# The recurrence's convolution and gates as float32 products on TensorE, on unsplit data

## The chip, the cores and the metric

The kernel runs on one core of a Trainium2 chip. The metric is the device time of one execution in microseconds (us). The core has four compute engines that matter here: TensorE (PE, with PEld for its weight loads), VectorE (DVE), ScalarE (ACT) and GpSimd (POOL); SyncE (SP) issues the transfers. Each engine takes its instructions in the order of its own queue.

## What is computed

One step of a layer with two groups of heads that share one input: `x + W_out [a recurrence | sparse attention](norm(x) W_in)`, then `x + SwiGLU(norm(x))`. There are 1024 new rows of one stream and 8 x 16 rows of eight running streams, together 1152 rows in 9 tiles of 128, with a width of 1024. Cut to what the change touches, the recurrence is:

```python
def causal_conv(xr, prev, w, b):
    xpad = jnp.concatenate([prev, xr], axis=1)
    y = b
    for j in range(4):
        y = y + xpad[:, j:j + T] * w[j]          # one weight per tap and channel
    return y, xpad[:, -3:]

def rglru(x, pos, h_prev, ...):                  # x = causal_conv(...), 512 channels in 8 blocks of 64
    r = sigmoid(x_block @ w_rg + b_rg)
    i = sigmoid(x_block @ w_ig + b_ig)
    a = exp(-8 * r * softplus(-lru_lambda))
    h = scan(a, sqrt(1 - a * a) * i * x)         # along time, from h_prev
```

The other group takes queries, keys and values with rotary embedding, an indexer that scores every key, the best 256 (or a quarter) of them for every row, and softmax attention over those.

## The kernel before

Everything is held with channels or rows on the 128 partitions. Large products are split: a float32 operand becomes a high and a low part in the reduced type `fp32r`, and a product is three matmuls (`mm3`: high with high and the two mixed ones). `mm4` (line 207 on) is one float32 matmul on unsplit operands; before the change a few products of the index stage (`ps<-yF`) use it.

The stages follow one another: norm and k/v projections (to 71 us in the profiled execution), indexer scores (to 184), the recurrence ("lru", to about 389 with its tail), the query projection (`q_proj`, to 435), the recurrence's half of the output projection (`out_tile` with key "wa", to 500), attention (to 682), the attention half of the output ("wb", to 742) and the feed-forward part.

The recurrence runs in eight units, for each of 4 columns of 128 channels one `lru_main` ("m") and one `lru_gate` ("g"). A unit goes over the 1152 rows in 3 thirds of 384. In `lru_main` a third t is projected (24 `fp32r` matmuls, `ps<-h,w`), ACT copies the result to `xp` behind the three rows ahead of it (t = 2 holds 256 rows of the long stream and eight short streams of 16 rows, each with its own three rows), ACT writes tap 3 and the bias to `xc`, and DVE adds taps 0 to 2 with one `scalar_tensor_tensor` each (six in t = 2). `split` then makes `xh`: the high part on ACT, the low part on POOL. The gate weights come by DMA to `braw` and are split to `bd` on POOL. `gates` makes two `mm3` products `ps<-xh,bd` for a third, ACT makes `tr`, `ti`, `tt` from them, DVE and ACT work these into the coefficients, and three scans on DVE (`tr<-tt,tr,ti`) close a column and write its last state to `tail`. Tiles `xc`, `ti`, `tt` come from one ring of 8 (`LRU_C`); a column uses nine, so that those of one column wait for the scans of the column before.

`lru_out` transposes `tail` on PE (`ps<-ident,tail`) after the last column, and DVE copies the result to `to`. `q_proj` has 18 units of 24 matmuls (`ps<-w,h`), 432 in all; `out_tile` "wa" has 216 matmuls (`ps<-w,rest`, `ps<-smr,rest`, `ps<-rest`).

Beside these stages run side jobs. `topk` finds thresholds by counting: for one group of tiles ACT counts (with Sign), for the other DVE counts (`jk<-key,tk_cnt`), and DVE does the arithmetic between the counts (`tk_cand`, `tk_cnt`) and at last the masks. `k_rope` turns the keys (`kn<-kn,tab`, `rp<-kn`, `kn<-kn,rp`, `kn<-kn,kss`, 9 tiles), writes them out and stacks their transposes; its scratch (`gk`, `tab`, `rp`) lies in pool "woa" of the phase "wa". A planner (`run`, `step`, `fill`) sets the order in which the program is written; top-k steps are written with a priority lowered by 400. Then the program is scheduled anew by list scheduling, `TileContext(nc, schedule_with_timeline_sim=True)`, which sets each engine's final order. Pools of SBUF are stacks: a pool opened later takes the place of one that was closed, and what is written there waits for the last use of what lay there.

Of the kernel before, what the change touches and what calls it, by code (L numbers as in the profile page):

```python
# [9 lines left out]
F32 = mybir.dt.float32  # L10
F32R = mybir.dt.float32r
# [3 lines left out]
AF = mybir.ActivationFunctionType  # L15
# [66 lines left out]
class Kernel:  # L82
# [124 lines left out]
    def mm4(self, out, lhsT, rhs, start, stop):  # L207

        self.pe += 4 * rhs.shape[1] / 2400.0
        self.nc.tensor.matmul(out, lhsT, rhs, start=start, stop=stop)  # L210
# [192 lines left out]
    XH = 3  # L403
    XP = 2
    BD = 1
# [623 lines left out]
    def lru_main(self, n, c, lp):  # L1029
# [8 lines left out]
        braw = self.raw.tile([128, 2, 128], F32, tag="raw", name="braw")  # L1038
        nc.gpsimd.memset(braw, 0.0)
        for k, nm in ((0, "w_rg"), (1, "w_ig")):  # L1040
            for s in range(2):
                nc.sync.dma_start(braw[64 * s:64 * s + 64, k, 64 * s:64 * s + 64], I[nm][2 * c + s])
        bd = lp.tile([128, 2, 2, 128], F32R, tag="bd", name="bd", bufs=self.BD)
        self.hi(bd[:, :, 0, :], braw, "pool")
        self.lo(bd[:, :, 1, :], braw, bd[:, :, 0, :], "pool")
        xps, xhs, xcs, G = [], [], [], []
        trs = []

        def claim(k):
            while self.c_free < k:  # L1050
                yield 0.3
            self.c_free -= k

        def conv(t, px):
            self.begin()
            xc = third("xc")
            xcs.append(xc)
# [7 lines left out]
            xs = xp[:, 259:411].rearrange("p (b j) -> p b j", b=NB)  # L1065
            if t == 2:
                S.activation(xs[:, :, 3:19], px[:, 256:384].rearrange("p (b j) -> p b j", b=NB), AF.Copy)
                nc.gpsimd.tensor_scalar(xs[:, :, 0:3], prm[:, c, 16:40].rearrange("p (b j) -> p b j", b=NB), 1.0, 0.0,
                                        op0=ALU.mult, op1=ALU.add)
            xps.append(xp)  # L1070
            S.activation(xc, px[:, :384], AF.Identity, scale=prm[:, c, 3:4], bias=prm[:, c, 4:5])
            for j in range(3):
                wj = prm[:, c, j:j + 1]
                o = xc[:, :n]
                V.scalar_tensor_tensor(o, xp[:, j:j + n], wj, o, op0=ALU.mult, op1=ALU.add)
                if t == 2:
                    o = xc[:, 256:384].rearrange("p (b j) -> p b j", b=NB)
                    V.scalar_tensor_tensor(o, xs[:, :, j:j + 16], wj, o, op0=ALU.mult, op1=ALU.add)
            if t == 2:
                nc.gpsimd.tensor_scalar(tail[:, c, 0:3], xp[:, 256:259], 1.0, 0.0, op0=ALU.mult, op1=ALU.add)  # L1080
                nc.gpsimd.tensor_scalar(tail[:, c, 3:27].rearrange("p (b j) -> p b j", b=NB), xs[:, :, 16:19], 1.0, 0.0,
                                        op0=ALU.mult, op1=ALU.add)
            xh = lp.tile([128, 2, 384], F32R, tag="xh", name="xh", bufs=self.XH)
            self.split(xh, xc, "act", "pool")
            xhs.append(xh)
            return self.end() + self.LRU_LAT

        def gates(t):
            xh, xc = xhs[t], xcs[t]
# [4 lines left out]
            for k, dst in ((0, tr), (1, ti)):  # L1094
                pg = self.ps()
                self.mm3(pg[:, :384], bd[:, k, 0, :], bd[:, k, 1, :], xh[:, 0], xh[:, 1], True, True)
                S.activation(dst, pg[:, :384], AF.Tanh, scale=0.5, bias=hb[:, c, k:k + 1])
# [5 lines left out]
        for t in range(3):  # L1103
            px = self.ps()
            yield from self.proj_T(px[:, :384], w, self.h[t])
            yield from claim(1)
            ready.append(conv(t, px))
# [638 lines left out]
```

## Time and profile before

| | us |
|---|---|
| median of 3 runs (1569.49 to 1570.11) | 1569.83 |
| the profiled execution, its own time | 1569.72 |
| its span (1.8 us lie around it) | 1567.9 |
| PE busy in the span | 1446.7 |
| DVE busy | 916.7 |
| ACT busy | 626.2 |
| POOL busy | 312.8 |

The page gives the busy time of each engine, the span in 40 slices (39.2 us each) with the busy share in tenths, and the chain of work that ended last. PE bears 72% of that chain and DVE 18%. The slices tell which engine is full where: slices 5 to 12 (about 196 to 510 us) are DVE's, the rest is PE's.

### The profile page before, as it was taken

The page shows a single profiled execution, that of the slowest core. Times are in us where ns is not written, and L with a number is a line of the kernel's source. Part 1 is how long each engine was busy: PE and PEld are TensorE (multiplying, and loading weights), DVE is VectorE, ACT ScalarE, POOL GpSimd, SP SyncE. Part 2 cuts the span into 40 slices and gives each one's busy share as a digit, 9 for nine tenths or more (in the row PEclk, how much of TensorE's full clock was granted, in tenths as well). Part 3 has the DMA queues.
Part 4 walks back from the last instruction along what each step waited for, and adds up shares of the span by engine and source line. Part 5 has one row for each costly group of instructions (what it writes and reads, how often), then busy time and mean ns, then how long its engine had stood idle before and what let it go on. Part 6 is the DMA issues. An engine that isn't in the chain of part 4 may idle for free.

```text
span 1567.9 us, 20857 instructions
## 1 busy us (share of the span) xinstructions
PE 1446.7 (92%) x7754; PEld 1322.8 (84%) x7754; DVE 916.7 (58%) x1957; ACT 626.2 (40%) x1481; POOL 312.8 (20%) x453
## 2 busy tenths in 40 slices
PE   6889887756888999999999999999999999999998
PEld 6777777746766788888999999999898989898987
DVE  7556899999999888768324233333324242424143
ACT  6457968875633978655302020202120212111110
POOL 4215225541986434400000000000000000000000
PEclk8999898877898999999999999999999999999999
DMA  7201101100320002121202020202020201111003
GB/s 239 56 16 42 35 16 29 29 27 14 134 71 22 1 14 57 39 68 42 81 13 81 1 81 0 81 0 81 1 81 15 67 28 54 41 41 54 28 1 121
DMA packets 93797, 74.65 MB, mean 48 GB/s; under 512 B 13236, under 2 KB 84532, under 8 KB 93696
## 3 DMA queue, kind: packets, MB, share of 16 engines
q1 hardware_dynamic: 93696, 73.32, 15.5%
q8 instruction: 61, 1.00, 0.3%
q14 instruction: 40, 0.33, 0.1%
HBM read 67.03 MB, written 6.27 MB: 47 GB/s over the span
## 4 chain that ended last, share of the span: by engine, by line
PE 72%; DVE 18%; ACT 4%; issue 3%; DMA 1%; POOL 1%; SPq 0%; POOLq 0%; ACTq 0%; DVEq 0%
PE ps L205 67%; DVE jk L66 7%; PE ps L215 4%; DVE tk_cand L66 2%; DVE tr L66 1%; DVE xc L66 1%; ACT jk L66 1%; DVE qn L66 1%; DVE ti L66 1%; PE ps L210 1%; DVE tk_cnt L66 1%; DVE s L66 1%; DVE kn L66 0%; ACT relu L66 0%; DVE acc L66 0%
## 5 line engine op out<-in xcount | busy, mean ns | idle before, releaser
L205 PE MATMUL ps<-hf,w 128*128 128x384 f32 x2556 | 460.6, 338 | 0.0
L205 PEld LDWEIGHTS ps<-hf,w 128*128 128x128 f32 x2556 | 451.5, 187 | 0.8
L205 PE MATMUL ps<-w,a 128*128 128x512 f32 x999 | 239.1, 390 | 0.0
L66 DVE TENSOR_TENSOR acc<-ps,acc 128x512 f32<-128x512 f32 x234 | 161.3, 690 | 119.7 <-PE ps L205 119.2
L205 PEld LDWEIGHTS ps<-w,a 128*128 128x128 f32 x999 | 187.3, 188 | 40.1
L66 DVE TENSOR_TENSOR sg<-ps,sg 128x384 f32<-128x384 f32 x66 | 36.8, 557 | 281.7 <-PE ps L205 281.1
L66 ACT ACTIVATE w<-raw 128x512 fp32r<-128x512 f32 x128 | 77.7, 629 | 300.9 <-PE ps L205 220.0
L66 DVE TENSOR_TENSOR w<-raw,w 128x512 fp32r<-128x512 f32 x116 | 76.8, 688 | 85.0 <-ACT w L66 84.9
L66 ACT ACTIVATE a<-sg 128x384 fp32r<-128x384 f32 x66 | 34.5, 523 | 222.1 <-DVE sg L66 222.1
L66 ACT ACTIVATE jk<-s,tk_cand 128x384 bf16<-128x384 f32 (+3 forms) x128 | 99.8, 779 | 40.7 <-DVE tk_cand L66 36.8
L205 PE MATMUL ps<-hf,rest 128*128 128x384 f32 x612 | 114.5, 334 | 0.0
L205 PE MATMUL ps<-w,h 128*128 128x256 f32 (+1 forms) x600 | 102.6, 332 | 11.6 <-ACT sq L66 7.8
L205 PE MATMUL ps<-h,w 128*128 128x384 f32 x576 | 108.5, 348 | 0.5 <-ACT relu L66 0.5
L205 PEld LDWEIGHTS ps<-h,w 128*128 128x128 f32 x576 | 106.6, 198 | 0.6 <-ACT relu L66 0.6
L205 PEld LDWEIGHTS ps<-hf,rest 128*128 128x128 f32 x612 | 106.9, 188 | 0.2
L205 PEld LDWEIGHTS ps<-w,h 128*128 128x128 f32 x600 | 90.1, 207 | 18.3 <-ACT sq L66 8.2
L205 PE MATMUL ps<-w,rest 128*128 128x512 f32 x324 | 83.2, 406 | 11.3 <-POOL rest L66 11.1
L205 PEld LDWEIGHTS ps<-w,rest 128*128 128x128 f32 x324 | 61.0, 193 | 26.3 <-POOL rest L66 12.7
L66 ACT ACTIVATE sg<-ps 128x384 f32<-128x384 f32 x66 | 32.0, 485 | 121.3 <-PE ps L205 121.3
L205 PE MATMUL ps<-xh,bd 128*128 128x384 f32 x72 | 22.0, 426 | 46.3 <-ACT xh L66 40.6
L66 POOL TENSOR_SCALAR m<-m,mx 128x128 f32<-128x128 f32 (+7 forms) x64 | 47.5, 748 | 67.4 <-DVE mx L66 60.3
L205 PEld LDWEIGHTS ps<-xh,bd 128*128 128x128 f32 x72 | 15.1, 234 | 51.0 <-ACT xh L66 43.0
(263 smaller groups left out, 2221.0 us busy)
## 6 DMA issues: line engine op xcount, KB each, us to landing
raw<-in_w_ffn_in_dram SPq DMA_DIRECT2D x44, 512.0 KB, 3.9
raw<-in_w_ffn_out_dram SPq DMA_DIRECT2D x22, 512.0 KB, 3.6
raw<-in_w_in_dram SPq DMA_DIRECT2D x16, 512.0 KB, 5.1
out_dram<-acc SPq DMA_DIRECT2D x9, 512.0 KB, 2.6
x<-in_x_prompt_dram SPq DMA_DIRECT2D x8, 512.0 KB
acc<-in_x_prompt_dram SPq DMA_DIRECT2D x8, 512.0 KB, 4.2
tab<-in_rope_dram SPq DMA_DIRECT2D x34, 64.0 KB, 1.9
raw<-in_w_out_dram SPq DMA_DIRECT2D x4, 512.0 KB, 3.5
```

The source lines that it names most:

```text
L66: return f(*args, **kw)
L205: self.nc.tensor.matmul(out, lhsT, rhs, start=start, stop=stop)
L210: self.nc.tensor.matmul(out, lhsT, rhs, start=start, stop=stop)
L215: self.nc.tensor.transpose(out, in_, self.ident[0:n, 0:n])
```

## The change

The convolution becomes a product. For each column 16 ACT instructions in all (four a column) write four diagonal matrices `taps` (the identity scaled by one tap's weights), and four float32 matmuls `ps<-xp,taps` of 384 columns (in t = 2 four of 256 and four of 128) add up the taps in PSUM; ACT adds the bias on the way to `xc`. The gates take `xc` and `bd` unsplit, with one float32 matmul for each of two gates and a third. The ring `xh`, the staging tile `braw`, the split of `bd` and the DVE instructions of the convolution are gone; `bd` has two buffers instead of one. The copies to `xp` (`streams`) are written ahead of the claim of a tile for `xc`. The planner's cost of an `mm4` counts all dimensions of its operand.

```diff
--- before.py
+++ after.py
@@ -206,7 +206,7 @@
 
     def mm4(self, out, lhsT, rhs, start, stop):
 
-        self.pe += 4 * rhs.shape[1] / 2400.0
+        self.pe += 4 * np.prod(rhs.shape[1:]) / 2400.0
         self.nc.tensor.matmul(out, lhsT, rhs, start=start, stop=stop)
 
     def tr(self, out, in_):
@@ -400,9 +400,8 @@
     WA_HE = 'act'
     WB_HE = 'act'
     LAG = 1
-    XH = 3
     XP = 2
-    BD = 1
+    BD = 2
     LRU_HE = ('pool', 'pool', 'pool', 'pool', 'pool', 'pool', 'pool', 'pool')
     Q_HE = 'pool'
     W_NORM = 3
@@ -1035,15 +1034,16 @@
         prm, hb, sp2, m4, tail = self.prm, self.hb, self.sp2, self.m4, self.tail
         w, = yield from self.wait_w(("lru", n))
         third = lambda nm: lp.tile([128, 384], F32, tag="c", name=nm, bufs=self.LRU_C)
-        braw = self.raw.tile([128, 2, 128], F32, tag="raw", name="braw")
-        nc.gpsimd.memset(braw, 0.0)
+        bd = lp.tile([128, 2, 128], F32, tag="bd", name="bd", bufs=self.BD)
+        nc.gpsimd.memset(bd, 0.0)
         for k, nm in ((0, "w_rg"), (1, "w_ig")):
             for s in range(2):
-                nc.sync.dma_start(braw[64 * s:64 * s + 64, k, 64 * s:64 * s + 64], I[nm][2 * c + s])
-        bd = lp.tile([128, 2, 2, 128], F32R, tag="bd", name="bd", bufs=self.BD)
-        self.hi(bd[:, :, 0, :], braw, "pool")
-        self.lo(bd[:, :, 1, :], braw, bd[:, :, 0, :], "pool")
-        xps, xhs, xcs, G = [], [], [], []
+                nc.sync.dma_start(bd[64 * s:64 * s + 64, k, 64 * s:64 * s + 64], I[nm][2 * c + s])
+
+        taps = lp.tile([128, 4, 128], F32, tag="taps", name="taps", bufs=2)
+        for j in range(4):
+            S.activation(taps[:, j, :], self.ident, AF.Identity, scale=prm[:, c, j:j + 1])
+        xps, xcs, G = [], [], []
         trs = []
 
         def claim(k):
@@ -1051,10 +1051,9 @@
                 yield 0.3
             self.c_free -= k
 
-        def conv(t, px):
+        def streams(t, px):
+
             self.begin()
-            xc = third("xc")
-            xcs.append(xc)
             n = 384 if t < 2 else 256
             xp = lp.tile([128, 411], F32, tag="xp", name="xp", bufs=self.XP)
             if t == 0:
@@ -1062,38 +1061,42 @@
             else:
                 nc.gpsimd.tensor_scalar(xp[:, 0:3], xps[-1][:, 384:387], 1.0, 0.0, op0=ALU.mult, op1=ALU.add)
             S.activation(xp[:, 3:3 + n], px[:, :n], AF.Copy)
-            xs = xp[:, 259:411].rearrange("p (b j) -> p b j", b=NB)
             if t == 2:
+                xs = xp[:, 259:411].rearrange("p (b j) -> p b j", b=NB)
                 S.activation(xs[:, :, 3:19], px[:, 256:384].rearrange("p (b j) -> p b j", b=NB), AF.Copy)
                 nc.gpsimd.tensor_scalar(xs[:, :, 0:3], prm[:, c, 16:40].rearrange("p (b j) -> p b j", b=NB), 1.0, 0.0,
                                         op0=ALU.mult, op1=ALU.add)
-            xps.append(xp)
-            S.activation(xc, px[:, :384], AF.Identity, scale=prm[:, c, 3:4], bias=prm[:, c, 4:5])
-            for j in range(3):
-                wj = prm[:, c, j:j + 1]
-                o = xc[:, :n]
-                V.scalar_tensor_tensor(o, xp[:, j:j + n], wj, o, op0=ALU.mult, op1=ALU.add)
-                if t == 2:
-                    o = xc[:, 256:384].rearrange("p (b j) -> p b j", b=NB)
-                    V.scalar_tensor_tensor(o, xs[:, :, j:j + 16], wj, o, op0=ALU.mult, op1=ALU.add)
-            if t == 2:
                 nc.gpsimd.tensor_scalar(tail[:, c, 0:3], xp[:, 256:259], 1.0, 0.0, op0=ALU.mult, op1=ALU.add)
                 nc.gpsimd.tensor_scalar(tail[:, c, 3:27].rearrange("p (b j) -> p b j", b=NB), xs[:, :, 16:19], 1.0, 0.0,
                                         op0=ALU.mult, op1=ALU.add)
-            xh = lp.tile([128, 2, 384], F32R, tag="xh", name="xh", bufs=self.XH)
-            self.split(xh, xc, "act", "pool")
-            xhs.append(xh)
+            xps.append(xp)
+            return self.end()
+
+        def conv(t):
+            self.begin()
+            xp, n = xps[t], 384 if t < 2 else 256
+            pc = self.ps()
+            for j in range(4):
+                self.mm4(pc[:, :n], taps[:, j, :], xp[:, j:j + n], j == 0, j == 3)
+            if t == 2:
+                xs = xp[:, 259:411].rearrange("p (b j) -> p b j", b=NB)
+                for j in range(4):
+                    self.mm4(pc[:, 256:384].rearrange("p (b j) -> p b j", b=NB), taps[:, j, :], xs[:, :, j:j + 16],
+                             j == 0, j == 3)
+            xc = third("xc")
+            xcs.append(xc)
+            S.activation(xc, pc[:, :384], AF.Identity, bias=prm[:, c, 4:5])
             return self.end() + self.LRU_LAT
 
         def gates(t):
-            xh, xc = xhs[t], xcs[t]
+            xc = xcs[t]
             if not t:
                 trs.append(lp.tile([128, 1152], F32, tag="tr", name="tr", bufs=2))
             tr, ti, tt = trs[0][:, 384 * t:384 * t + 384], third("ti"), third("tt")
             G.append((tr, ti, tt))
             for k, dst in ((0, tr), (1, ti)):
                 pg = self.ps()
-                self.mm3(pg[:, :384], bd[:, k, 0, :], bd[:, k, 1, :], xh[:, 0], xh[:, 1], True, True)
+                self.mm4(pg[:, :384], bd[:, k, :], xc, True, True)
                 S.activation(dst, pg[:, :384], AF.Tanh, scale=0.5, bias=hb[:, c, k:k + 1])
             S.activation(tt, tr, AF.Tanh, scale=sp2[:, c:c + 1], bias=sp2[:, c:c + 1])
             V.scalar_tensor_tensor(ti, ti, 1.0, xc, op0=ALU.add, op1=ALU.mult)
@@ -1103,8 +1106,9 @@
         for t in range(3):
             px = self.ps()
             yield from self.proj_T(px[:, :384], w, self.h[t])
+            yield from self.until(streams(t, px))
             yield from claim(1)
-            ready.append(conv(t, px))
+            ready.append(conv(t))
             yield 0.0
             yield from claim(2)
             while not t and not self.tr_free:
```

The scheduler's order changes with it. On PE, at the end of the recurrence (`h_0` and `h_1` with a number are high and low parts of the normed input's thirds): before, the last gates stand among the first rows of the query projection.

```order
L205 MATMUL ps<-h_0_97,w 128x384 x12
L205 MATMUL ps<-h_1_98,w 128x384 x12
L205 MATMUL ps<-xh,bd 128x384 x2
L205 MATMUL ps<-h_0_99,w 128x384 x4
L205 MATMUL ps<-xh,bd 128x384 x4
L205 MATMUL ps<-h_0_99,w 128x384 x8
L205 MATMUL ps<-h_1_100,w 128x384 x12
L205 MATMUL ps<-xh,bd 128x384 x8
L205 MATMUL ps<-w,h_0_95 128x256 x12
L205 MATMUL ps<-w,h_1_96 128x256 x7
L205 MATMUL ps<-xh,bd 128x384 x4
```

And after:

```order
L210 MATMUL ps<-xp,taps 128x384 x4
L205 MATMUL ps<-h_0_97,w 128x384 x12
L205 MATMUL ps<-h_1_98,w 128x384 x12
L210 MATMUL ps<-xp,taps 128x384 x4
L210 MATMUL ps<-xc,bd 128x384 x2
L205 MATMUL ps<-h_0_99,w 128x384 x12
L205 MATMUL ps<-h_1_100,w 128x384 x12
L210 MATMUL ps<-xp,taps 128x256 x4
L210 MATMUL ps<-xc,bd 128x384 x2
L210 MATMUL ps<-xp,taps 128x128 x4
L210 MATMUL ps<-xc,bd 128x384 x2
L205 MATMUL ps<-w,h_0_95 128x256 x12
```

The convolution's products stand ahead of the gates of the last column, and the whole query projection stands behind the last gates. From there to the last transpose of `tail` 152 of its 432 matmuls are written, and 280 behind it.

On DVE, around the copy `to` that closes the recurrence (`jk`, `key`, `tk_cand`, `tk_cnt` and `s_8..` are the top-k search, `qn` the queries' rotation), before:

```order
L66 TENSOR_SCALAR tk_cand<-tk_cnt 128x3
L66 SCALAR_TENSOR_TENSOR tk_cnt<-tk_cand,tk_cnt 128x3
L66 TENSOR_SCALAR jk_911,tk_cnt<-key,tk_cnt 128x896
L66 COPY to<-ps 36x512
L66 TENSOR_SCALAR jk_911,tk_cnt<-key,tk_cnt 128x1024
L66 TENSOR_SCALAR jk_911,tk_cnt<-key,tk_cnt 128x528
L66 TENSOR_SCALAR tk_cand<-tk_cnt 128x3
L66 RECIPROCAL nr_4398<-nr_4398 128x18
L66 SCALAR_TENSOR_TENSOR tk_cnt<-tk_cand,tk_cnt 128x3
L66 TENSOR_TENSOR nr_4399<-nr_4399,nr_4398 128x18
L66 TENSOR_SCALAR jk_911,tk_cnt<-key,tk_cnt 128x896
L66 TENSOR_TENSOR nr_4399<-nr_4399,nr_4398 128x18
```

And after:

```order
L66 COPY tail<-tr 128x1
L66 COPY tail<-tr 128x8
L66 TENSOR_TENSOR tk_cnt<-tk_cnt 128x4
L66 SCALAR_TENSOR_TENSOR tk_cnt<-tk_cnt 128x4
L66 TENSOR_SCALAR tk_cnt<-tk_cnt 128x4
L66 TENSOR_TENSOR tk_cnt<-tk_cnt 128x4
L66 TENSOR_SCALAR jk_912<-s_888,tk_cnt 128x384
L66 TENSOR_SCALAR s_888,tk_cnt<-s_888,tk_cnt 128x384
L66 TENSOR_SCALAR tk_cnt<-tk_cnt 128x1
L66 COPY to<-ps 36x512
L66 TENSOR_TENSOR qn<-qn,tab 128x256
L66 TENSOR_TENSOR qn<-qn,rp 128x256
```

Before, the search goes on behind `to` and between the queries' rotations; after, all but one group of its last masks stands ahead of `to`, and the queries' rotations follow one another.

On DVE, the keys' rotation (`kn`), before, in the stage "wa":

```order
L66 TENSOR_SCALAR s_892,tk_cnt<-s_892,tk_cnt 128x896
L66 TENSOR_TENSOR kn<-kn,tab 128x128
L66 TENSOR_TENSOR qn<-qn,tab 128x256
L66 TENSOR_SCALAR tk_cnt<-tk_cnt 128x1
L66 TENSOR_TENSOR kn<-kn,rp 128x128
L66 TENSOR_TENSOR qn<-qn,rp 128x256
L66 SCALAR_TENSOR_TENSOR jk_911<-key,tk_cnt,jk_911 128x896
L66 TENSOR_TENSOR qn<-qn,tab 128x256
L66 TENSOR_TENSOR qn<-qn,rp 128x256
```

And after, among the norms of the first stage:

```order
L66 SCALAR_TENSOR_TENSOR x<-x,ss,gmix 128x1024
L66 TENSOR_TENSOR h_1_96<-ps,h_1_96 128x4x128
L66 TENSOR_TENSOR kn<-kn,tab 128x128
L66 TENSOR_TENSOR h_0_95<-ps,h_0_95 128x4x128
L66 TENSOR_TENSOR h_1_96<-ps,h_1_96 128x4x128
L66 RECIPROCAL nr_484<-nr_484 128x1
L66 TENSOR_TENSOR kn<-kn,rp 128x128
L66 TENSOR_TENSOR h_0_97<-ps,h_0_97 128x4x128
```

With the ring `xh` gone the pool "lru" takes less of SBUF (by the tiles' shapes about 32 KB of a partition instead of 37), and the scratch of `k_rope` no longer lies where "lru" was. All of its 18 DVE instructions, its 36 on POOL, its loads of `gk` and `tab` and its stores now stand in the first stage; the stacking of the transposed keys stays where it was.

## Rows read from the trace of the kernel before

**Rows 1.** The page: busy us of each engine, then busy tenths in 40 slices.
```profile
PE 1446.7 (92%) x7754; PEld 1322.8 (84%) x7754; DVE 916.7 (58%) x1957; ACT 626.2 (40%) x1481; POOL 312.8 (20%) x453
...
DVE  7556899999999888768324233333324242424143
```

**Rows 2.** Stretches of the span: start:end, length; busy us of PE, PEld, DVE, ACT, POOL; granted clock.
```profile
0.00:71.40 71.40, 52.71 (x330) 49.77 (x330) 49.15 (x128) 40.11 (x116) 29.44 (x57) 0.93 0.51 160
...
183.60:360.40 176.80, 130.52 (x668) 125.75 (x669) 172.68 (x429) 137.35 (x271) 75.31 (x103) 0.86 0.10 26
...
388.60:434.70 46.10, 37.60 (x265) 37.19 (x266) 45.65 (x86) 30.55 (x154) 40.17 (x52) 0.83 0.38 126
434.70:500.50 65.80, 54.70 (x222) 42.95 (x222) 63.73 (x127) 16.92 (x75) 55.18 (x72) 0.92 0.16 49
```

**Rows 3.** Groups by form, 185 to 390 us: busy us, mean ns, idle before.
```profile
L205 PE MATMUL ps<-xh,bd 128*128 128x384 f32 x72 | 22.0, 426 | 46.3 <-ACT xh L66 40.6 <-POOL xh L66 4.5 <-POOL xp L66 1.1
...
L66 DVE SCALAR_TENSOR_TENSOR xc<-xp,prm,xc 128x384 f32<-128x384 f32 x24 | 16.1, 671 | 0.0
...
L66 POOL TENSOR_TENSOR xh<-xc,xh 128x384 fp32r<-128x384 f32 x12 | 12.7, 1060 | 21.6 <-ACT xh L66 21.4
...
L66 ACT ACTIVATE xh<-xc 128x384 fp32r<-128x384 f32 x12 | 6.3, 522 | 15.2 <-DVE xc L66 15.1
...
L66 DVE SCALAR_TENSOR_TENSOR xc<-xp,prm,xc 128x256 f32<-128x256 f32 x12 | 5.7, 476 | 0.0
...
L66 DVE SCALAR_TENSOR_TENSOR xc<-xp,prm,xc 128x128 f32<-128x128 f32 x12 | 4.9, 404 | 0.0
```

**Rows 4.** Timeline of PE: start us, length us, instructions; a float32 product and fp32r ones.
```profile
121.81 1.50 PE L210 MATMUL ps<-yF 128*128 128x264 f32 x6
...
217.66 5.05 PE L205 MATMUL ps<-h,w 128*128 128x384 f32 x28
```

**Rows 5.** Instructions of line 210 (float32): ns least/median/most, first and last start.
```profile
L210 PEld LDWEIGHTS ps<-yF x32: 186/188/317, 121.7 to 177.6; 128*128 128x128 f32 x32
L210 PE MATMUL ps<-yF x32: 383/385/490, 121.8 to 177.8; 128*128 128x264 f32 x32
```

**Rows 6.** Timeline of PE, end of the recurrence, with the idle time ahead in brackets.
```profile
359.45 1.07 PE L205 MATMUL ps<-xh,bd 128*128 128x384 f32 x4
360.36 14.88 PE L205 MATMUL ps<-w,h 128*128 128x256 f32 x125
...
385.14 0.40 PE L215 MATMUL ps<-ident,tail 128*36 128x128 f32 x1 [6.74 <-DVE tail L66]
389.32 2.93 PE L205 MATMUL ps<-w,h 128*128 128x256 f32 x12 [3.79 <-DVE to L66]
```

**Rows 7.** Timeline of PE, the stage "wa" and the first product of attention.
```profile
440.20 2.96 PE L205 MATMUL ps<-w,rest 128*128 128x512 f32 x12
...
471.97 2.93 PE L205 MATMUL ps<-w,rest 128*128 128x512 f32 x6 [7.23 <-POOL rest L66]
...
505.75 0.44 PE L205 MATMUL ps<-k,qeo 128*128 128x128 f32 x2 [2.53 <-DVE qeo L66]
```

**Rows 8.** Waits, 385 to 510 us: total, times, longest.
```profile
ACT jk L66 <- DVE tk_cand L66: 15.7, 3, 6.6
...
PE ps L205 <- POOL rest L66: 11.1, 4, 7.2
...
PE ps L205 <- ACT sq L66: 7.8, 2, 5.8
```

**Rows 9.** Stretch from `to` on, instructions that name `jk` alone (DVE, ACT, POOL).
```profile
388.60:510.00 121.40, 0.00 (x0) 40.99 (x58) 16.27 (x36) 10.41 (x7) 0.88 0.24 77
```

**Rows 10.** Groups of DVE by form, 388.6 to 510 us: a small step of the search.
```profile
L66 DVE SCALAR_TENSOR_TENSOR tk_cand<-tk_cand 128x4 int32<-128x4 int32 x5 | 3.9, 777 | 0.0
```

**Rows 11.** DVE's rotation of the keys (`kn`): ns least/median/most, first and last start.
```profile
L66 DVE TENSOR_TENSOR kn<-kn,tab x9: 282/546/1131, 416.2 to 499.9; 128x128 f32<-128x128 f32 x9
L66 DVE TENSOR_TENSOR kn<-kn,rp x9: 279/543/1323, 417.9 to 500.2; 128x128 f32<-128x128 f32 x9
```

## The prediction

> **What bounds the kernel now.** I read the page first, then stretches of the span, then groups by form where the change lies, then PE's timeline around the end of the recurrence. PE is the engine of the whole (1446.7 of 1567.9 us), but the DVE slices at 9 and 8 from about 196 to 510 us say that the middle is not PE's [rows 1]. By stretch, DVE is busy for 172.7 of the 176.8 us to 360.4, for 45.7 of the 46.1 from 388.6 and for 63.7 of the 65.8 of stage "wa", while PE has 130.5, 37.6 and 54.7 [rows 2]. So an instruction taken off DVE there can shorten the run; one added to PE in the recurrence costs nothing until PE's room is gone. Two places tie PE to DVE. Ahead of the gates PE idles for 46.3 us, 40.6 of it released by ACT's `xh`, which itself waits 15.1 us for DVE's `xc` [rows 3]. At the end of the recurrence PE runs ahead of DVE, waits 6.7 us for `tail` and 3.8 us for `to` [rows 6]. From there the path is query projection, stage "wa", attention: 389.3 us to the first product of attention at 505.75 [rows 6, 7].
>
> **The convolution leaves DVE.** Its 48 instructions take 16.1 + 5.7 + 4.9 = 26.7 us [rows 3]. That is the gain on the bound engine. ACT's 12 `xh` (6.3 us) and POOL's 12 (12.7 us) go too [rows 3]; neither bounds, but they stand in the chain to the gates. ACT receives 16 small `taps`; the stretch has over 35 us of idle ACT [rows 2], so I count them at nothing. If that cover were gone they would cost 16 times some 0.3 to 0.5 us, 5 to 8 us.
>
> **What PE receives.** A float32 product is seen in the index stage: each matmul has two records of a load and a product (32 records for 16 instructions), and six records took 1.50 us, so (1.50 - 0.385) / 5 = 0.223 us a record and 0.446 us for 264 columns [rows 4, 5], or 1.69 ns a column. By columns a product of 384 costs 0.65 us, of 256 0.43 and of 128 0.22; the last cannot be under its two loads of 0.188 us [rows 5], so 0.38. A column of channels has 8 of 384, 4 of 256 and 4 of 128: 5.2 + 1.7 + 0.9 to 1.5 = 7.8 to 8.4 us, four times that 31 to 34 us. The gates change from 72 `fp32r` matmuls at (5.05 - 0.35) / 27 = 0.174 us [rows 4], 12.5 us, to 24 of 0.65, 15.6 us. Together PE receives 34 to 37 us. From the start of the recurrence to the last gates it has 130.5 us of work now [rows 2], so some 165 to 168, where I expect about 194 us to pass (below): hidden, with 26 us of room. The Trainium skill, "FP8 and Floating Point Precision", section "TensorE Precision Notes", speaks against the gates' part: true float32 takes four passes, where the split product made three; by it the gates cost 12.5 x 4 / 3 = 16.7 us, 4 us more than now, against 3 by the row, an estimate that leaves the room at 25 us.
>
> **What DVE receives instead.** The order of the change shows it: nearly all of the top-k search that ran behind `to` now stands ahead of it. Behind `to`, instructions naming `jk` had 41.0 us of DVE [rows 9]; about 6 of them remain there, so 35 us come forward, and with the small steps between the counts (the largest group 3.9 us, [rows 10]) 41 us. So `to` moves by -26.7 + 35 to 41 = +8 to +14 us; I take +14, as the small steps cannot be left behind.
>
> **The keys' rotation goes to the first stage.** With the smaller pool its memory no longer waits for the recurrence. On DVE it had 9 x 0.546 + 9 x 0.543 = 9.8 us by medians, 5.0 us by the shortest (9 x 0.282 + 9 x 0.279) [rows 11]; 36 POOL instructions go with it, in the order of the change. In the first stage DVE is busy for 49 of 71 us and POOL for 29 [rows 2], so there is room, but the loads of `gk` and `tab` are queued on SP among those of the weights, and a norm may stand behind a `kn` that waits. I bound this between 0 and 5 us and take 2. What leaves the "wa" stage is what stood there beside the waits: PE waited 11.1 us for POOL's `rest` [rows 8], in a stretch in which POOL was busy for 55 of 66 us [rows 2].
>
> **The sum.** `to` releases PE at 389.3 now [rows 6]; with +14 and +2 at about 405. The last gates need a tile of the ring, which the second scan of the third column frees; by after's order and before's durations about 27 us of DVE work stand between that scan and `to` (28 us lie between gates and `to` now, [rows 6]), so the last gates end near 378. Behind them come 152 matmuls of the query projection at (14.88 - 0.30) / 124 = 0.118 us [rows 6], 18 us, to 396. `tail` is ready some 4 us ahead of `to`, at 401: a stall of 5 us where there are 10.5 now. Then 280 matmuls, 33 us: 434. Now the same stretch has 7.8 us of waiting for ACT's `sq` [rows 8], because ACT's counts stood in the queue (`jk` waited 15.7 us for `tk_cand`, [rows 8]); these counts now come before. A lower clock behind the stall may remain: the 12 matmuls at 389.3 took (2.93 - 0.3) / 11 = 0.24 us each [rows 6], and the granted clock of that stretch is 0.83 of full speed [rows 2], part of it at the lower of its two levels (1.2 and 2.4 GHz). For both I add 4 us (0 to 8): "wa" starts at 438, against 434.7. "wa" itself is 216 matmuls at (2.96 - 0.41) / 11 = 0.232 us [rows 7], 50 us, where 65.8 are taken now [rows 2]. The single stall of 7.2 us [rows 7] and its kin stood beside POOL's and DVE's `kn`; 3 us (1 to 6) of them remain in my sum: 491. The first product of attention comes 5.2 us behind "wa" now, of which 2.5 are a wait for DVE's `qeo` [rows 7]; DVE has no search left there, and I take 4.5: 495.5 against 505.75, so -10. Nothing behind that changes its order to speak of. The profiled execution took 1569.72 us, practically the median of 1569.83: 1569.7 - 10.2 = 1559.5.
>
> **Ends of the range.** Low: the hoisted rotation costs nothing, DVE works a little faster beside a POOL with less to do, `to` at 397, no clock loss: -24, 1546. High: `to` at 412, 8 us of clock and waits, 6 in "wa": +4, 1574.
>
> **Rivals.** *The search in front costs more than it weighs.* Placed ahead of `to`, DVE's `tk_cand` and ACT's counts hand work to each other, and DVE takes its queue in order: where it must wait for a count, the recurrence's scans stand behind it. ACT already waits for `tk_cand` in long pieces (6.6 us, [rows 8]). The recurrence is DVE work of some 215 us; each per cent idle there is 2 us. It decides at `to` near 415 (26 us later than now, 5% idle); with 10% idle `to` is at 426 and the time 1581. For it: a search of 41 us is put in front of PE's last gates. Against it: DVE was 98% busy with the same kind of mixture [rows 2]. *No change:* "wa" keeps its stalls because POOL's `rest`, not the keys, makes them. Then it lasts 65.8 us and the sum is 1569.7 - 10.2 + 12.6 = 1572 at the worst; with half of them, 1566; the cases within 0.2% lie between. *The whole of DVE's saving counts:* 26.7 and the 9.8 us of the keys' rotation come off, 1533. Against it stands that PE needs 18 + 33 + 50 = 101 us behind the last gates whatever DVE does. *DVE works faster beside an emptier POOL:* the same `kn` on DVE takes from 0.282 to 1.131 us [rows 11] in a stretch that POOL fills to five sixths [rows 2]. If DVE got back all of POOL's 12.7 us of `xh` [rows 3], `to` would be at 392 and the time 1547; but POOL is busy for only 75 of 177 us in the recurrence [rows 2], and most of its work stays. The Trainium skill, "SBUF — State Buffer", section "SBUF: two separate sides", says that a POOL instruction and a DVE one with two SBUF inputs exclude each other; the spread of `kn` agrees with it. *PE becomes the bound of the recurrence:* were the float32 products twice as dear, PE would have some 213 us of work before the last gates, 19 more than the 194 that I expect to pass, and the time would be 1578. For it only that convolution and gates are small pieces with waits between; the room of 26 us is against it.
>
> **How the numbers follow.** A comparison tells about 0.2%, 3 us. The forecast, 1550 to 1566.5, has 0.58; a larger gain, by the faster DVE or the whole saving, 0.12; no change within 3 us 0.13; the search in front 0.12; PE as bound 0.05. That is 0.70 faster, 0.13 same, 0.17 slower. The range of 1546 to 1574 leaves about 0.05 below (the whole saving) and 0.11 above.
>
> **What would show it.** Right: DVE's busy time falls by about 23 to 30 us; no `kn` on DVE past 75 us; `to` at 400 to 410, the last gates at 373 to 383; "wa" in 51 to 56 us with waits for `rest` under 6; first product of attention near 495; the stretches from attention on as long as before. Wrong: `to` past 415 or DVE under 93% busy in the recurrence; waits for `rest` as before; a start of the recurrence later by over 5 us; PE without idle time ahead of the gates.

## The result: slower by 1%

The changed kernel takes 1585.9 us at the median (1582.8 to 1587.5) against 1569.7 us: a ratio of 1.0095 with an interval of 1.0083 to 1.0107. Forecast was 1559.5, with a range to 1574. The profiled execution is its fastest, 1582.8 us with a span of 1580.7, so the traces show 12.8 us of the 16.

The page of the changed kernel, busy us of each engine and then PE's and DVE's slices (for [rows 1]):

```profile
PE 1477.3 (93%) x7858; PEld 1335.3 (84%) x7858; DVE 886.4 (56%) x1909; ACT 624.4 (39%) x1484; POOL 288.7 (18%) x433
...
PE   6899898875989899999999999999999999999998
...
DVE  7656899998676887768424242423333242424143
```

DVE lost 30.3 us, as intended, and PE received 30.6. The slices say that DVE is no longer full from 400 us on. To see where the time went, the span is cut at three events: the arrival of the recurrence's parameters (`prm` on DVE), the end of the last gates on PE, and the first product of attention. First the stretches of before (start:end, length, then busy us of PE, PEld, DVE, ACT, POOL, and the granted clock):

```profile
189.60:360.50 170.90, 124.63 (x636) 119.86 (x636) 167.32 (x418) 131.37 (x259) 75.20 (x103) 0.85 0.10 26
360.50:505.70 145.20, 112.77 (x655) 99.56 (x653) 142.09 (x292) 67.34 (x277) 104.35 (x135) 0.88 0.20 65
505.70:1567.90 1062.20, 1047.71 (x5644) 967.11 (x5644) 479.04 (x982) 307.59 (x651) 69.80 (x94) 0.99 0.14 43
```

And those of the changed kernel:

```profile
193.10:397.00 203.90, 157.57 (x722) 132.91 (x721) 192.81 (x481) 146.79 (x309) 68.82 (x90) 0.91 0.07 20
397.00:517.40 120.40, 108.42 (x675) 96.48 (x673) 81.20 (x157) 49.27 (x230) 73.17 (x93) 0.96 0.21 68
517.40:1580.70 1063.30, 1048.78 (x5644) 968.13 (x5644) 478.77 (x982) 307.93 (x651) 69.97 (x94) 0.99 0.14 43
```

The recurrence starts 3.5 us later, takes 33.0 us longer to its last gates, and the stretch from there to attention is 24.8 us shorter; the remaining 1.1 us lie behind. The first row of each is the case in short. Before, PE is busy for 124.6 of 170.9 us and idle for 46.3. After, it is busy for 157.6 of 203.9 and idle for 46.3 again. PE received 33.0 us of work, and the stretch grew by 33.0 us. By this count nothing of it was hidden. The count alone doesn't name the cause: in the same rows DVE's busy time grew by 25.5 us, with search that stood later in the kernel before. The experiments have to tell the two apart.

What ACT and PE waited for in that stretch of the changed kernel (total us, times, longest):

```profile
ACT jk L66 <- DVE tk_cand L66: 48.3, 18, 5.6
...
PE ps L210 <- ACT xp L66: 37.7, 9, 8.9
...
PE ps L210 <- ACT xc L66: 8.6, 3, 3.8
```

Where PE waited 40.6 us for ACT's `xh` and 5.6 for POOL [rows 3], it now waits 37.7 for ACT's `xp` and 8.6 for ACT's `xc`: another name and the same length. ACT itself waits 48.3 us with a count of the search (`jk`) for DVE's arithmetic (`tk_cand`); before, in its own stretch, this was 14.1:

```profile
ACT jk L66 <- DVE tk_cand L66: 14.1, 8, 4.2
```

How that reaches PE is seen ahead of the last column's third convolution, on ACT:

```profile
386.67 0.61 ACT L66 ACTIVATE jk<-s,tk_cand 128x384 bf16<-128x384 f32 x1 [5.61 <-DVE tk_cand L66]
...
388.13 0.54 ACT L66 ACTIVATE xp<-ps 128x256 f32<-128x256 f32 x2
```

The copies to `xp` need nothing of the search, but they stand behind a count that waits 5.6 us for DVE. Not every wait of PE is of this kind. From 362.7 to 370.8 us PE stands still once more for an `xp`, and there ACT, the fourth busy time of the row, works for 7.18 of 8.10 us: counts of the search, table loads and steps of the recurrence itself stand ahead of the copy.

```profile
362.70:370.80 8.10, 0.03 (x1) 0.06 (x1) 8.10 (x9) 7.18 (x14) 6.97 (x7) 0.80 0.22 66
```

On PE the moment of the first case, and the steps behind it (start us, length, idle time ahead in brackets; for [rows 6, 7]):

```profile
388.64 3.38 PE L210 MATMUL ps<-xp,taps 128*128 128x256 f32 x8 [7.77 <-ACT xp L66]
...
395.45 1.56 PE L210 MATMUL ps<-xc,bd 128*128 128x384 f32 x4 [1.25 <-ACT xc L66]
396.55 17.42 PE L205 MATMUL ps<-w,h 128*128 128x256 f32 x144
...
418.35 31.36 PE L205 MATMUL ps<-w,h 128*128 128x256 f32 x264 [0.65 <-DVE to L66]
449.55 2.92 PE L205 MATMUL ps<-w,rest 128*128 128x512 f32 x12
...
464.46 2.93 PE L205 MATMUL ps<-w,rest 128*128 128x512 f32 x6 [3.71 <-POOL rest L66]
...
517.36 0.44 PE L205 MATMUL ps<-k,qeo 128*128 128x128 f32 x2 [2.98 <-DVE qeo L66]
```

From the last gates on, the query projection runs without a stall to speak of, and the stage "wa" takes 63 us.

### The profile page after: what moved, and what is told of

It reads as the page before. It is cut to its first block, busy times and chain, and to the rows that moved or that the text cites. A ratio compares the mean times of both kernels' runs of the same rounds, so it can differ in the third digit from the quotient of the medians.

```text
span 1580.7 us, 21030 instructions
## 1 busy us (share of the span) xinstructions
PE 1477.3 (93%) x7858; PEld 1335.3 (84%) x7858; DVE 886.4 (56%) x1909; ACT 624.4 (39%) x1484; POOL 288.7 (18%) x433
## 3 DMA queue, kind: packets, MB, share of 16 engines
q1 hardware_dynamic: 93696, 73.32, 15.5%
## 4 chain that ended last, share of the span: by engine, by line
PE 72%; DVE 15%; ACT 5%; POOL 3%; issue 3%; DMA 1%; SPq 0%; POOLq 0%; ACTq 0%; DVEq 0%
PE ps L205 67%; DVE jk L66 7%; PE ps L215 3%; DVE tk_cand L66 2%; ACT jk L66 1%; DVE tr L66 1%; POOL rp L66 1%; PE ps L210 1%; DVE ti L66 1%; POOL qn L66 1%; DVE s L66 1%; ACT qeo L66 1%; ACT m L66 1%; ACT relu L66 0%; DMA tab<-in_rope_dram 0%
## 5 line engine op out<-in xcount | busy, mean ns | idle before, releaser
L205 PEld LDWEIGHTS ps<-h,w 128*128 128x128 f32 x576 | 102.3, 190 | 4.7 <-ACT relu L66 0.6
L205 PE MATMUL ps<-w,h 128*128 128x256 f32 (+1 forms) x600 | 94.6, 314 | 0.6 <-DVE to L66 0.6
L205 PEld LDWEIGHTS ps<-w,h 128*128 128x128 f32 x600 | 82.2, 188 | 7.3 <-DVE to L66 0.9
L210 PE MATMUL ps<-xp,taps 128*128 128x384 f32 (+2 forms) x128 | 44.5, 504 | 37.7 <-ACT xp L66 37.7
L210 PEld LDWEIGHTS ps<-xp,taps 128*128 128x128 f32 x128 | 26.7, 231 | 51.7 <-issue 43.8
```

## Experiments

The tables of stretches below all run from `prm` to the end of the last gates. PE's idle time is the length less PE's busy time.

**The search held back.** The first theory was the first rival of the prediction: the search in front delays the recurrence. Two kernels tie part of it to the recurrence's own states, so that it must come later.

```diff
             for b in range(15, -1, -1):
+                if b == 15:
+                    while 2 not in self.hs:
+                        yield 1.0
+                    nc.vector.scalar_tensor_tensor(t, self.tail[:, 2, 28:28 + g["n"]], 0.0, t, op0=ALU.mult, op1=ALU.add)
                 yield from self.topk_count(g, t, True)
```

> The changed kernel, but the low sixteen counting rounds of the DVE search are tied to the third column's last state (they read tail, times zero), so that they cannot stand ahead of its scans; some 42 us of the search move back behind `to`. Theory A (the search pulled ahead of the recurrence delays it, on DVE and through ACT's queue): `to` falls from 417.6 to 375 to 395 us and the kernel to 1550 to 1570. Theory B (the float32 products lie in PE's chain and set the recurrence's pace): `to` stays above 408 and the time within 8 us of the changed kernel's 1586.

Measured: 1595.1 us, 1.0152 (1.0136 to 1.0167) of before: slower still. The second kernel holds from b == 7 on, for column 3.

> As the first, but only the last eight counting rounds are held, and until the fourth column's last state; the first eight still stand ahead. Theory A: `to` between that of the first experiment and the changed kernel's 417.6, near 385 to 400, and time 1555 to 1575. Theory B: as the changed kernel within 8 us.

Measured: 1592.6 us, 1.0138 (1.0121 to 1.0155). Of the first, the stretch:

```profile
193.80:382.20 188.40, 156.38 (x722) 132.38 (x722) 134.47 (x374) 151.17 (x319) 55.01 (x84) 0.93 0.08 22
```

And PE's largest wait between it and attention:

```profile
PE ps L205 <- POOL rest L66: 28.6, 4, 19.3
```

The recurrence itself became faster by 15.5 us: PE's work is the same (156.4 us), its idle time falls from 46.3 to 32.0. So the search in front has a share in the wait. But it isn't the whole (before needed 170.9), and with the search that was held back standing later, PE waits 28.6 us for POOL's `rest` in the stage "wa". `to` comes at 407.1 us in the first kernel and at 411.5 in the second. Theory A, that the order alone costs the time, falls: both times and both `to` lie outside its ranges. The first kernel just misses theory B's ranges too (407.1 against 408, 9 us from the changed kernel against 8), the second keeps them. Neither place for these 42 us of search was free.

**The keys' rotation.** One kernel puts the rotation back into the stage "wa" in the changed kernel, by 5 KB of unused memory; the other brings it forward in the kernel before.

```diff
+        pad = lp.tile([128, 1280], F32, name="pad")
+        nc.gpsimd.memset(pad[:, 0:1], 0.0)
```

> The changed kernel with 5 KB a partition of unused memory in the recurrence's pool, so that its size is that of before and the keys' rotation goes back to the stage wa; order around the recurrence unchanged. Theory C (the rotation's move to the first stage costs the time): the recurrence starts at 189 to 190 us in place of 193.1 and the time falls by 3 us or more. Theories A and B: `to` moves by those 3 to 4 us at most, the stage wa grows by 3 to 12 us, so the time is 1582 to 1596.

Measured: 1589.9 us, 1.0119 (1.0104 to 1.0134).

```diff
-    XH = 3
+    XH = 2
```

> The kernel before with two buffers for xh instead of three, whose smaller pool lets the keys' rotation go to the first stage, as in the changed kernel; the rest of the order is that of before. Theory C: slower than before by 3 us or more, with the start of the recurrence 3 to 4 us later. Theories A and B: the start comes 3 to 4 us later, the stage wa has less of POOL and DVE to wait for, and the time is 1558 to 1572.

Measured: 1570.0 us, 0.9994 (0.9984 to 1.0003). The move costs nothing in the kernel before and saves some 4 us in the changed one. `prm` comes at 190.2 us with the rotation put back and at 193.9 where it was brought forward: the 3 to 4 us at the start are the rotation's, and the later stages give them back. Theory C falls.

**The two halves.** First the convolution alone on PE, with the split and the three products for the gates as before (the split of `bd` comes back with it; dots stand for lines that are not shown):

```diff
...
             S.activation(xc, pc[:, :384], AF.Identity, bias=prm[:, c, 4:5])
+            xh = lp.tile([128, 2, 384], F32R, tag="xh", name="xh", bufs=self.XH)
+            self.split(xh, xc, "act", "pool")
...
-                self.mm4(pg[:, :384], bd[:, k, :], xc, True, True)
+                self.mm3(pg[:, :384], bd[:, k, 0, :], bd[:, k, 1, :], xh[:, 0], xh[:, 1], True, True)
```

> One half of the change: the convolution as float32 products on PE, but xc split to xh on ACT and POOL and the gates as three fp32r products, as before. If the convolution is what slows (both theories), within 6 us of the changed kernel's 1586 or slower, as the split comes on top; if the gates are, near 1570.

Measured: 1580.2 us, 1.0059 (1.0044 to 1.0074). Then the gates alone, with DVE's convolution as before (the split of `bd` goes with that of `xc`):

```diff
...
-        self.split(xh, xc, "act", "pool")
...
-                self.mm3(pg[:, :384], bd[:, k, 0, :], bd[:, k, 1, :], xh[:, 0], xh[:, 1], True, True)
+                self.mm4(pg[:, :384], bd[:, k, :], xc, True, True)
```

> The other half of the change: the convolution stays on DVE, only the gates become float32 products on unsplit xc. PE receives about 3 us, DVE nothing, POOL loses 17 us, ACT 6 us, the split leaves the path to the gates, and the keys' rotation moves to the first stage. If the convolution's price on PE is the whole of the loss: 1558 to 1570, no slower than before. If the unsplit gates share in it: 1573 or more.

Measured: 1570.4 us, 0.9994 (0.9985 to 1.0003). The unsplit gates alone change nothing that can be measured (1570.4 lies at the edge of the first range), although POOL's busy time on the page falls from 312.8 to 285.5 us and ACT's from 626.2 to 621.5; the convolution alone costs. Its stretch is that of the whole change, and that of the gates alone is shorter than before. The first, then the second:

```profile
191.00:397.60 206.60, 159.13 (x772) 143.10 (x771) 193.23 (x481) 146.03 (x314) 86.30 (x109) 0.89 0.08 22
```

```profile
194.30:358.50 164.20, 122.35 (x594) 110.52 (x593) 161.15 (x419) 130.16 (x257) 56.81 (x84) 0.86 0.09 25
```

**The price of the convolution on PE.** One kernel makes it cheap, the other doubles it. Cheap, by `fp32r` tiles, which gives the convolution less precision:

```diff
-        taps = lp.tile([128, 4, 128], F32, tag="taps", name="taps", bufs=2)
+        taps = lp.tile([128, 4, 128], F32R, tag="taps", name="taps", bufs=2)
...
-            xp = lp.tile([128, 411], F32, tag="xp", name="xp", bufs=self.XP)
+            xp = lp.tile([128, 411], F32R, tag="xp", name="xp", bufs=self.XP)
```

> The changed kernel with xp and taps in fp32r, so that each tap is one reduced product, with less precision in the convolution; the price on PE falls from some 32 us to some 12. Theory B: prm to last gates falls from 202 us by 10 to 25, and the time from 1586 to 1562 to 1578. Theory A: the search still stands in front and the time stays within 6 us of 1586.

Measured: 1564.7 us, 0.9957 (0.9940 to 0.9973). It is 21 us faster than the changed kernel and 0.4% faster than the kernel before, with less precision. Doubled, but for the products of 128 columns:

```diff
+            for j in range(4):
+                nc.tensor.matmul(pc[:, :n], taps[:, j, :], xp[:, j:j + n], start=j == 0, stop=j == 3)
             for j in range(4):
                 self.mm4(pc[:, :n], taps[:, j, :], xp[:, j:j + n], j == 0, j == 3)
```

> The changed kernel with the four tap products of every third issued twice into the same PSUM tile (the second round starts anew, so the result is the same): 48 float32 products more on PE, about 26 us of work by the measured 0.65 and 0.43 us, and nothing on the other engines. If PE's idle ahead of the gates is no room (it waits for copies on ACT that do not come earlier or later by PE's own pace): prm to the last gates grows from 204 us by 20 to 28. If there is room: by less than 8.

Measured: 1607.3 us, 1.0227 (1.0208 to 1.0246). The stretches, cheap and then doubled:

```profile
195.20:364.90 169.70, 135.24 (x658) 122.22 (x657) 165.45 (x444) 132.00 (x274) 54.46 (x84) 0.88 0.09 24
```

```profile
196.30:419.60 223.30, 183.59 (x818) 149.74 (x817) 193.12 (x505) 150.33 (x318) 67.55 (x90) 0.92 0.07 18
```

PE's work goes from 157.6 us to 135.2 and to 183.6, by -22.3 and +26.0; the stretch goes by -34.2 and +19.4. So three quarters of what is added on PE lengthen the recurrence (just under the 20 us that were named as the least), and what is taken away shortens it by more than itself, and by more than theory B's 10 to 25 us. The doubled kernel keeps the changed kernel's amount of search in front of `to`, so its 19.4 us are the price of PE's work alone. The cheap one's order also leaves some 10 us of the search behind `to` (in front of it stand 167 us in the changed kernel and 156 in the cheap one, summed over DVE's instructions of the search in the traces), and its idle time falls by 11.8 us: price and order are not told apart there.

**What the wait is made of.** Four kernels leave out most of the search's counting, so that the selection is coarse; only the recurrence's stretch is read. First the changed kernel and the kernel before without most of either group's rounds:

```diff
-        for b in range(31, last - 1, -1):
+        for b in range(31, 27 if g["act"] else 29, -1):
...
-            for b in range(15, -1, -1):
+            for b in range(15, 13, -1):
```

> The changed kernel with most of the search's counting rounds left out (4 of 32 on ACT, 2 of 16 and 2 of 16 on DVE), so its selection is coarse and its time is not that of the whole work; what is left shows the recurrence's own pace. To be read against the next run. Theory B (the convolution and gates as float32 products lengthen the recurrence's chain PE, ACT, PE, ACT): from prm to the last gates this takes 10 us or more longer than the next run. Theory A (only the search in front delays): not longer, rather 10 to 25 us shorter, as DVE has 26.7 us less to do.

> The kernel before with the same rounds of the search left out; the other side of the comparison. From prm to the last gates I expect 100 to 140 us, by the DVE work that remains (some 120 us by the order's sum).

Measured: 1548.0 us for the changed kernel, 1544.0 for the kernel before. The stretches:

```profile
209.80:365.50 155.70, 141.68 (x707) 124.01 (x706) 85.09 (x180) 67.47 (x111) 70.00 (x92) 0.96 0.10 26
```

```profile
206.70:361.30 154.60, 120.48 (x627) 116.93 (x626) 126.54 (x228) 69.52 (x108) 96.81 (x111) 0.88 0.11 29
```

In both, `prm` arrives later than in the whole kernels, with more of the projection's products ahead of it, the same number in both; so they are read against each other. With most of the search left out, the change costs 1.1 us in this stretch: PE's work grows by 21.2 us and its idle time falls from 34.1 to 14.0. This is how I had thought of PE's room, and here it is there. The 1.1 us are a balance, since DVE's work falls by 41.5 us at the same time. Theory B, that the new chain of products is longer by itself by 10 us or more, falls as well, and theory A's 10 to 25 us shorter did not come either. My length for the kernel before (100 to 140 us) was too short. Then only one group's rounds are left out. With few rounds on ACT:

```diff
-        for b in range(31, last - 1, -1):
+        for b in range(31, 27 if g["act"] else last - 1, -1):
```

> The changed kernel with 4 of 32 counting rounds left on ACT (the selection of tiles 2 to 5 is coarse); DVE's own counting is whole. If ACT's counts, waiting for DVE's arithmetic, are what holds the copies that PE waits for: PE's idle between prm and the last gates falls from 46 us to under 25, and the last gates come 20 us or more earlier after prm. If DVE's load is what holds the recurrence: idle stays over 38 us.

Measured: 1592.7 us. The stretch:

```profile
210.20:399.90 189.70, 146.38 (x707) 125.78 (x706) 182.03 (x409) 65.33 (x109) 54.42 (x79) 0.90 0.07 19
```

And two of its waits (the ACT instruction without a name is the table load ahead of the recurrence's own steps):

```profile
ACT L66 <- DVE tr L66: 47.0, 3, 20.7
PE ps L210 <- ACT xp L66: 42.6, 6, 22.0
```

Idle time is 43.3 us, almost what it was. The stretch is 14 us shorter, but only because it starts 17 us later, as `prm` does, with 15 more of the projection's products ahead of it: the last gates end at 399.9 us, where the changed kernel's end at 397.0. The wait only changed its place: with most of the counts gone, ACT waits 47.0 us ahead of the recurrence's own exponentials and roots for DVE's `tr`, which stands behind the search in DVE's queue. With few rounds on DVE instead (the edit of the low and high rounds above, for that group alone):

> The changed kernel with DVE's own counting cut to 2 of 16 and 2 of 16 rounds (the selection of tiles 6 to 8 is coarse); ACT's 32 rounds are whole, so ACT keeps its queue. Theory D (the search standing in DVE's queue ahead of the recurrence's own instructions keeps ACT's copies late, whichever instruction of ACT waits): PE's idle between prm and the last gates falls from 46 us to under 25 and the stretch from 204 us to under 180, with PE's busy time near 150. Theory A' (ACT's own counts are what holds the copies): idle stays over 38 us.

Measured: 1562.1 us. The stretch:

```profile
195.60:374.10 178.50, 152.91 (x722) 130.47 (x721) 101.40 (x264) 149.01 (x318) 67.81 (x90) 0.94 0.08 23
```

And a wait of DVE and one of PE in it:

```profile
DVE tk_cand L66 <- ACT jk L66: 43.5, 15, 5.1
...
PE ps L210 <- ACT xp L66: 24.9, 8, 5.6
```

Idle time falls to 25.6 us, just outside the "under 25" of theory D, and the stretch to 178.5, just inside its 180; theory A' had said over 38. So it is mainly DVE's queue, filled by the search, that holds ACT's copies, through whichever ACT instruction waits for DVE ahead of them. ACT's own counts have a share, too: here DVE waits 43.5 us for them, and when they go as well (few rounds on both), PE's idle falls from 25.6 to 14.0 us. Taken away alone, as above, they returned 3.0. With DVE 95% busy (192.8 of 203.9 us) PE's idle is 46.3 us; with 71% (the search held) 32.0, with 57% (few rounds on DVE) 25.6, with 55% (few rounds on both) 14.0. All four have the changed kernel's convolution and gates.

## Why the prediction was wrong

**DVE's saving: right.** DVE's busy time fell by 30.3 us on the page, where 23 to 30 were named. From `prm` to `to` it rose; the row of before, and that of the changed kernel:

```profile
189.60:388.60 199.00, 142.93 (x787) 137.63 (x786) 195.10 (x487) 146.63 (x296) 81.05 (x111) 0.85 0.08 23
```

```profile
193.10:417.60 224.50, 177.87 (x892) 152.90 (x890) 209.20 (x522) 157.51 (x334) 74.09 (x98) 0.92 0.07 18
```

From 195.1 to 209.2 us of work, +14.1, and +14 was the term of the sum. The search did come forward and more than refill what the convolution left. What the sum didn't have is idle time of DVE: length less busy time, it was 3.9 us in the first row and is 15.3 in the second. These 11.4 us, with a start that came 3.5 us later instead of 2, put `to` at 417.6 instead of 405. DVE's largest waits in the second row:

```profile
DVE ti L66 <- ACT ti L66: 3.6, 3, 2.7
DVE tk_cand L66 <- ACT jk L66: 3.6, 2, 2.6
DVE tt L66 <- ACT tr L66: 2.6, 1, 2.6
```

The first and the last, 6.2 us, are waits for the recurrence's own gates.

**PE's price: right as a sum, not in its parts.** 34 to 37 us were worked out, 33.0 measured, but that is luck in part. The convolution's products were busy for 44.5 us of the stretch (first row: PE, PEld, ACT of the instructions that name `taps`) where 31 to 34 were worked out. Against it, the gates fell from 22.0 us [rows 3] to 19.6, where 3 us more were worked out, and the 4.7 us of the query projection that stood in the stretch before (second row) stand behind the last gates now. These times overlap at their edges and don't add up to the 33.0.

```profile
193.10:397.00 203.90, 44.51 (x128) 26.67 (x128) 4.97 (x16) 0.91 0.07 20
```

```profile
L205 PE MATMUL ps<-w,h 128*128 128x256 f32 x21 | 4.7, 402 | 0.0
```

The single product was right: of the two rows of four products (8 records) below, the first, undisturbed, gives (2.74 - 0.486) / 7 x 2 = 0.64 us for 384 columns, where 0.65 was worked out; 0.486 us is the median length of a record of that size, here by the gates' row. For 128 columns the prediction's lower bound of 0.38 us, by two loads, was wrong: with 0.273 us for a record, (1.05 - 0.273) / 7 x 2 = 0.22 us.

```profile
L210 PE MATMUL ps<-xc,bd x48: 483/486/847, 223.3 to 396.5; 128*128 128x384 f32 x48
```

```profile
393.14 1.05 PE L210 MATMUL ps<-xp,taps 128*128 128x128 f32 x8
```

What a wait ahead of the products costs besides its length:

```profile
355.78 2.74 PE L210 MATMUL ps<-xp,taps 128*128 128x384 f32 x8
...
370.77 4.64 PE L210 MATMUL ps<-xp,taps 128*128 128x384 f32 x8 [8.08 <-ACT xp L66]
```

The granted clock of those stretches (busy times of all engines ahead of it):

```profile
355.80:358.00 2.20, 2.20 (x8) 1.31 (x7) 2.20 (x2) 2.20 (x6) 2.12 (x3) 1.00 0.04 7
370.80:375.20 4.40, 4.40 (x8) 2.51 (x9) 4.40 (x13) 0.96 (x3) 1.07 (x4) 0.59 0.00 0
```

The first had the upper of the two levels (1.2 and 2.4 GHz) throughout, the second the lower one for most of its length, behind 8 us of idle PE. Before, such waits stood ahead of the gates; now most of them stand ahead of the convolution.

**The failed step is "hidden, with 26 us of room".** I compared PE's work (165 to 168 us) with the time that I expected to pass (194 us) and called the difference room. It was a wait for ACT, and behind it mostly for DVE's queue. Added work fills an idle time only if what the engine waits for comes no later on account of it. Here PE must deliver a third's projection, get `xp` back from ACT, deliver the convolution, get `xc`, and deliver the gates; each time ACT's copy can stand behind something of the search, which waits for DVE (48.3 us in the stretch) or works itself. The idle time stayed at 46.3 us, and the last gates ended at 397 instead of 378: 19 us, of which 1.5 are the later start. That added work isn't hidden is shown by the doubled convolution, where 19.4 of 26.0 us came through; that the search is what takes the room away, by the kernels with few rounds, where the whole change costs 1.1 us on balance. The rest of the sum held: 117.5 us were worked out from the last gates to attention, 120.4 measured (the projection had almost no stall and took 7 us less than worked out; "wa" took 63 instead of 53 with 8.0 us of waits for `rest`). With 19 + 3 us, and the 1 us behind, the forecast becomes 1582.5, which is the profiled execution.

**The step before that** is the reading that with DVE 98% busy "an instruction taken off DVE there can shorten the run". By the order and its durations some 130 of the 195 us were a side job that fills whatever is free. That share says nothing of what the recurrence needs: with most of the search left out, the kernel before still takes 154.6 us to the last gates with DVE busy for 126.5.

**The rivals.** "The search in front" named the place (`to` past 415, DVE under 93% busy) and came out at `to` 417.6 with DVE at 93.2%, the first sign met and the second just missed. But it is only a part of the cause: holding the search back returned 15.5 of the 33 us, and of DVE's waits only 3.6 us were for a count, the mechanism that it named. "PE as bound" named the other part and rejected it for the room that wasn't there. Both ends together had 0.17.

**What stays open.** How the 33 us divide between the search in front and PE's added work isn't shown; no kernel took one of them away and left the other as it was. That idle time is 46.3 us before and after is measured, but why it is so exactly the same isn't explained; it is 39.7 to 50.3 in the other kernels with the float32 convolution and the full search on DVE ahead of `to`. The unsplit gates cost some 9 to 10 us on top of the convolution (1589.9 against 1580.2 us, both with the rotation in the stage "wa") and nothing without it; most of that lies behind the last gates and wasn't pursued. A version with the changed kernel's exact order and a cheaper convolution wasn't tried.

## What to carry to other kernels

Idle time of an engine is room only if the thing that it waits for doesn't depend on it, or comes when it comes; where two engines hand work back and forth in order, added work can come on top of the wait, as three quarters of it did here. Before a busy share is called a bound, take out what merely fills the engine. And where a side job uses an engine too, the time that a change frees on it can go to the side job first: look in the new order for who moved in.

## What the runs showed of the hardware

Behind a wait of 8.08 us the clock was at its lower level for most of the next four products, so that the wait cost more than its length: they took 4.64 us, and 2.74 us in a row of work. The keys' rotation has no fixed price on DVE: `kn` takes 0.28 and 0.55 us at the least and the median beside the stage "wa" [rows 11], and in the first stage of the changed kernel, with POOL busy for 35.8 of 71.4 us, its median is near the least:

```profile
L66 DVE TENSOR_TENSOR kn<-kn,tab x9: 274/291/1375, 30.0 to 77.8; 128x128 f32<-128x128 f32 x9
L66 DVE TENSOR_TENSOR kn<-kn,rp x9: 265/280/292, 32.5 to 78.1; 128x128 f32<-128x128 f32 x9
```

It would be easy to put this down to POOL's share. But in the kernel before with few rounds of the search the rotation stood mostly beside the stage "wa" as well, with POOL, the last busy time of the second row, busy for 47.87 of 59.40 us, and its median was 0.29 us there, too. What makes it 0.55 us in the kernel before stays open.

```profile
L66 DVE TENSOR_TENSOR kn<-kn,tab x9: 292/292/1378, 402.3 to 461.7; 128x128 f32<-128x128 f32 x9
```

```profile
402.30:461.70 59.40, 44.61 (x221) 37.20 (x220) 35.99 (x68) 14.61 (x74) 47.87 (x76) 0.89 0.35 119
```
